# Output stage beside the last MoE: sums, scaling and roots change engine, fetches and list scatters change their waits

## The chip, the cores and the metric

One Trainium2 chip, one of its cores. The metric is the device time of one execution of the program, in microseconds, as the median of several runs; 1389.53 us for the kernel before. TensorE multiplies matrices into PSUM, VectorE and ScalarE work on PSUM and SBUF, GpSimd on SBUF alone; GpSimd also issues the indirect DMAs (gathers and scatters by a list of row numbers), SP the plain ones. Every engine works through its own instructions in order.

## The reference, cut to what matters

A trunk of two layers, 1024 tokens and 16 meta tokens, 1024 channels. Each layer ends in a mixture of experts: every token goes to 2 of 32 experts, and its two weighted results are added to its residual row. After the second layer comes one RMS norm, and the meta tokens are dropped.

```python
h = h + hierarchical_moe(rmsnorm(h, ffn_norm[layer]), ...)      # two experts a token
...
return rmsnorm(h, final_norm)[:, N_META:]

def rmsnorm(x, g):
    y = xf * lax.rsqrt(jnp.mean(xf * xf, axis=-1, keepdims=True) + RMS_EPS)
    return (y * g).astype(x.dtype)
```

## The kernel before, in words

The change lies in the second MoE, the last 400 us of the program. `Moe.run` takes the 32 experts in turn, in passes e = 0 to 32. For each expert, up to 96 tokens' rows are gathered from HBM (`gather`, L905, three passes ahead), turned (L923) and scaled into `xq` (L926), multiplied with gate and up weights (L950 in full precision for one half; L1558 to L1560 for the other, where weights and rows are split into a high and a low part, `wp` and `xT`, by ScalarE at L1553 and VectorE at L1554), passed through silu (ScalarE L974, VectorE L975, tile `hm`), turned again (L984, `ph`, split into `hT`), and multiplied with the down weights (`py`, again L1558 to L1560). VectorE adds the weighted result to the token's row (`rows`, L999), and GpSimd scatters it to `y_d` in HBM (L911), which has two rows a token, one for each of its experts. The passes overlap: pass e holds expert e's gate and up products and expert e-1's turn, down product, L999 and scatter. SP loads the weights into a ring of 17 slots (L895), three a pass, some five experts ahead.

`Out` forms the output rows beside this. Tokens are sorted by the later of their two experts; a list of them is made in passes 0 to 8 by `Router.order` (`later`, `masks`, `sums` on TensorE, `starts`, `places`, `suits`), eight scatters (`place_ids`, L844) and a load (`load_list`, on SP's queue with the weights). The sorted list is cut into seven tiles of 128 tokens. `EARLY_OUT` names the pass at which each tile is due; `suits` counts what is not complete by then, and `again` does everything over where the count is not zero. For tiles 0 to 4, due at pass f:

- `begin(f)`: two gathers fetch the two rows of each token from `y_d` (`fetch`, L1187). The scatters are not ordered among themselves, but the fetch waits for those issued before it.
- `begin(f+1)`: GpSimd adds the two rows (`add`, L1212); `middle(f+1)`: ScalarE squares and sums them (`square`, L1215), ahead of the pass's silu; `end(f+1)`: VectorE takes the root (`root`, L1219 and lines 173 to 183, a start by bits and three steps of refinement).
- `begin(f+2)`: GpSimd multiplies by the gain (`gain`, L1224); `middle(f+2)`: ScalarE multiplies by the root (`scale`, L1227).
- `begin(f+3)`: a scatter writes the tile to the output (`store`, L1197).

Tiles 5 and 6 come in passes 29 to 32. The tokens of the last three experts (`DIRECT`) are not fetched whole: `other` (L1205) fetches their other expert's row and adds it to the row that L999 has just made; `last` and `rest` write these three sets and tile 6 after the final expert.

`begin` stands in a pass right after the gather of three experts ahead, `middle` between the split of `xT` and the second half of the gate and up products, `end` after `hm`. The order of issue in the program is each engine's order of work.

Of the kernel before, what the change touches and what calls it, by code (L numbers as in the profile page):

```python
# [53 lines left out]
EARLY_OUT = (9, 13, 17, 21, 25, 29, 30)  # L54
# [115 lines left out]
def rsqrt_ops(k, y, ms, tmp):  # L170

    V = k.nc.vector
# [162 lines left out]
class Router:  # L335
# [440 lines left out]
    def order(self, psum, c):  # L776
# [9 lines left out]
        def later():  # L786
            V.tensor_tensor(w.rearrange("p (n e) -> p n e", e=NE), self.oh.rearrange("p n j e -> p (n j) e"),
                            k.iota32.unsqueeze(1).to_broadcast([128, 2 * n, NE]), op=OP.mult)
            V.tensor_reduce(self.later.unsqueeze(2), w.rearrange("p (n x) -> p n x", n=n), axis=AX.X, op=OP.max)
# [36 lines left out]
        def suits():  # L826
# [3 lines left out]
            for i, e in enumerate(EARLY_OUT):  # L830
                V.tensor_copy(lim[:, i:i + 1], st[:, e - 1:e])
# [47 lines left out]
class Moe:  # L879
# [121 lines left out]
    def run(self, loads, ahead):  # L1001
# [166 lines left out]
class Out:  # L1168
# [48 lines left out]
    def root(self, i, n=1):  # L1217
        st = self.st[:, :, i:i + n]
        self.k.nc.vector.tensor_scalar(st[:, 1], st[:, 0], 1.0 / D, EPS, op0=OP.mult, op1=OP.add)  # L1219
        for f in rsqrt_ops(self.k, st[:, 2], st[:, 1], st[:, 3]):  # L1220
            f()

    def gain(self, c, n=128):
        self.k.nc.gpsimd.tensor_tensor(c[0][:n], c[0][:n], self.g[:n], op=OP.mult)  # L1224
# [15 lines left out]
    def begin(self, e):  # L1240
        k, r, nc = self.k, self.r, self.k.nc
        later, masks, sums, starts, places, suits = self.order
# [7 lines left out]
        if 5 < e < 6 + DIRECT:  # L1250
            r.load_tokens(e - 6)
# [24 lines left out]
    def middle(self, e):  # L1276

        for f in EARLY_OUT[:-2]:
            if e == f + 1:
                self.square(self.a, 0)  # L1280
            if e == f + 2:
                self.scale(self.a, 0)
        if e == NE - 2:
            self.square(self.a, 0)
        if e == NE - 1:
            self.square(self.b, 1)
            self.square(self.rows(0), 2, CAP)

    def end(self, e):
        k, r = self.k, self.r  # L1290
        later, masks, sums, starts, places, suits = self.order
        if e == 0:
            k.nc.vector.memset(self.st, 1.0)
            k.nc.sync.dma_start(out=self.g, in_=bcast_row(k.A["final_norm"], D))
            later()
        if e == 1:
            masks()
        if e == 2:
            starts()
        if e == 3:  # L1300
            places()
        if e == 4:
            suits()
        if e == 8:
            r.lists()
        if e == 10:
            r.tokens()
        for f in EARLY_OUT[:-1]:
            if e == f + 1:
                self.root(0)  # L1310


    def last(self):

        self.scale(self.a, 0)
# [1334 lines left out]
```

## Time and profile before

| what | us |
|---|---|
| median of 3 runs (1387.86 to 1390.33) | 1389.53 |
| the profiled execution | 1388.98 |
| its span, first to last instruction | 1387.2 |
| TensorE busy in the span | 1279.1 (92%) |
| VectorE | 1071.8 (77%) |
| ScalarE | 756.4 (55%) |
| GpSimd | 391.1 (28%) |

The profile is of one execution. A row names the engine (PE for TensorE, PEld for its weight loads, DVE for VectorE, ACT for ScalarE, POOL for GpSimd, SP for SyncE), the line, the operation and the tiles (out<-in). Granted clock is the share of TensorE's full clock that the chip allowed. Shares of busy time are means over stages with different limits; what the change touches is read from the second MoE, 979 us to the end.

### The profile page before, as it was taken

The page shows a single profiled execution, that of the slowest core. Times are in us where ns is not written, and L with a number is a line of the kernel's source. Part 1 is how long each engine was busy: PE and PEld are TensorE (multiplying, and loading weights), DVE is VectorE, ACT ScalarE, POOL GpSimd, SP SyncE. Part 2 cuts the span into 40 slices and gives each one's busy share as a digit, 9 for nine tenths or more (in the row PEclk, how much of TensorE's full clock was granted, in tenths as well). Part 3 has the DMA queues.
Part 4 walks back from the last instruction along what each step waited for, and adds up shares of the span by engine and source line. Part 5 has one row for each costly group of instructions (what it writes and reads, how often), then busy time and mean ns, then how long its engine had stood idle before and what let it go on. Part 6 is the DMA issues. An engine that isn't in the chain of part 4 may idle for free. (4 is left out here: it accounts for less than half of the span.)

```text
span 1387.2 us, 22810 instructions
## 1 busy us (share of the span) xinstructions
PE 1279.1 (92%) x8029; PEld 1100.5 (79%) x8029; DVE 1071.8 (77%) x2529; ACT 756.4 (55%) x1603; POOL 391.1 (28%) x492
## 2 busy tenths in 40 slices
PE   8979999999997999999999999997899798898883
PEld 6977888888885899899888889896677677686672
DVE  5777888888887776776787676688788688787796
ACT  4435555556555555655665565563555455555553
POOL 0122212121210441122231232213215423323455
PEclk9999999999998999999999999997899999999996
DMA  8927999999963502132010010448596999998632
GB/s 310 396 109 242 371 348 368 352 357 356 351 206 103 196 1 69 48 146 90 20 39 9 12 39 1 167 150 341 192 300 241 385 365 341 355 371 309 220 99 75
DMA packets 81709, 293.12 MB, mean 211 GB/s; under 512 B 22896, under 2 KB 30320, under 8 KB 65074
## 3 DMA queue, kind: packets, MB, share of 16 engines
q1 hardware_dynamic: 63202, 245.54, 48.8%
q0 software_dynamic: 18384, 46.04, 9.9%
q8 instruction: 65, 1.06, 0.3%
q14 instruction: 58, 0.48, 0.1%
HBM read 270.75 MB, written 47.00 MB: 229 GB/s over the span
## 5 line engine op out<-in xcount | busy, mean ns | idle before, releaser
L1558 PE MATMUL gu<-wp,xT 128*96 128x256 f32 x512 | 147.3, 288 | 0.0
L1560 PE MATMUL gu<-wp,xT 128*96 128x256 f32 x512 | 143.4, 280 | 0.0
L1559 PE MATMUL gu<-wp,xT 128*96 128x256 f32 x512 | 143.3, 280 | 0.0
L1554 DVE TENSOR_TENSOR wp<-slotB,wp 128x512 fp32r<-128x512 f32 x160 | 106.9, 690 | 22.5 <-ACT wp L1553 21.6
L1558 PE MATMUL py<-wp,hT 128*96 128x512 f32 x256 | 115.9, 453 | 0.8 <-ACT hT L1553 0.8
L1559 PE MATMUL py<-wp,hT 128*96 128x512 f32 x256 | 104.3, 408 | 8.3 <-DVE wp L1554 8.3
L1560 PE MATMUL py<-wp,hT 128*96 128x512 f32 x256 | 105.3, 411 | 5.3 <-DVE hT L1554 4.9
L1553 ACT ACTIVATE wp<-slotB 128x512 fp32r<-128x512 f32 x160 | 96.0, 626 | 23.8 <-PE py L1560 20.2
L2461 POOL TENSOR_TENSOR hh<-hh,wt 128x512 f32<-128x512 f32 x56 | 72.5, 1294 | 111.4 <-ACT wt L2460 111.4
L1553 ACT ACTIVATE xT<-xq 128x384 fp32r<-128x384 f32 x64 | 33.7, 526 | 111.8 <-DVE xq L926 111.8
L911 POOL DMA_INDIRECT y_d<-xg,di x34 | 35.5, 1043 | 197.9 <-DVE xg L999 188.5
L1558 PEld LDWEIGHTS gu<-wp,xT 128*96 128x96 f32 x512 | 84.9, 166 | 0.1
L1560 PEld LDWEIGHTS gu<-wp,xT 128*96 128x96 f32 x512 | 83.2, 162 | 0.0
L1559 PEld LDWEIGHTS gu<-wp,xT 128*96 128x96 f32 x512 | 82.9, 162 | 0.2
L950 PE MATMUL gu<-slotB,xq 128*96 128x256 f32 x320 | 75.6, 379 | 0.0
L2297 ACT ACTIVATE P<-bank,sm 128x400 f32<-128x400 f32 (+3 forms) x112 | 59.6, 540 | 25.7 <-DVE sm L2287 25.5
L2050 DVE TENSOR_TENSOR T<-bank,T 128x512 fp32r<-128x512 f32 (+2 forms) x112 | 53.6, 495 | 20.8 <-ACT T L2046 19.8
L975 DVE SCALAR_TENSOR_TENSOR hm<-gu,table,hm 96x256 f32<-96x256 f32 x64 | 30.7, 480 | 49.3 <-ACT hm L974 49.3
L926 DVE TENSOR_TENSOR xq<-pt,ffg 128x768 f32<-128x768 f32 (+1 forms) x66 | 61.0, 926 | 9.8 <-PE pt L923 9.8
L1559 PEld LDWEIGHTS py<-wp,hT 128*96 128x96 f32 x256 | 42.7, 167 | 30.8 <-DVE wp L1554 13.7
L2464 DVE SCALAR_TENSOR_TENSOR hh<-bank,ri,hh 128x512 f32<-128x512 f32 x72 | 53.5, 746 | 16.9 <-PE bank L1560 16.4
L1560 PEld LDWEIGHTS py<-wp,hT 128*96 128x96 f32 x256 | 42.7, 167 | 27.1 <-DVE hT L1554 9.4
(444 smaller groups left out, 4060.6 us busy)
## 6 DMA issues: line engine op xcount, KB each, us to landing
slotB<-w_up SPq DMA_DIRECT2D x20, 1024.0 KB, 14.9
slotB<-w_down SPq DMA_DIRECT2D x20, 1024.0 KB, 16.0
slotB<-w_gate SPq DMA_DIRECT2D x20, 1024.0 KB, 16.2
hh<-w_gate SPq DMA_DIRECT2D x11, 1024.0 KB, 14.0
hh<-w_up SPq DMA_DIRECT2D x10, 1024.0 KB, 9.9
hh<-w_down SPq DMA_DIRECT2D x10, 1024.0 KB, 11.4
slotR<-w_gate SPq DMA_DIRECT2D x10, 1024.0 KB, 13.0
slotR<-w_up SPq DMA_DIRECT2D x10, 1024.0 KB, 10.2
```

The costliest lines, as they stand in the source:

```text
L911: return nc.gpsimd.indirect_dma_start(out=self.r.y_d, out_offset=bass.IndirectOffsetOnAxis(ap=didx, axis=0), in_=y[:CAP], in_offset=None, ...
L926: nc.vector.tensor_tensor(x[:, 4 * a:4 * (a + w)].rearrange("p (a b) c -> p a b c", a=w), pt[:, a:a + w].rearrange("p a (b c) -> p a b c", ...
L950: nc.tensor.matmul(gu[:CAP, f * FE:f * FE + FE], lhsT=x[0][:, j], rhs=w[:, j], start=(f == 0 and j == 0), stop=False)
L1553: nc.scalar.activation(dH, src, AF.Copy)
L1554: nc.vector.tensor_tensor(dL, src, dH.bitcast(F32), op=OP.subtract)
L1558: nc.tensor.matmul(out, lhsT=aH, rhs=bH, start=start, stop=False)
L1559: nc.tensor.matmul(out, lhsT=aH, rhs=bL, start=False, stop=False)
L1560: nc.tensor.matmul(out, lhsT=aL, rhs=bH, start=False, stop=stop)
L2050: nc.vector.tensor_tensor(dL, src, dH.bitcast(F32), op=OP.subtract)
L2297: nc.scalar.activation(self.P[hd, qp][a][:, x0:x0 + xe], tt[:, :xe], AF.Exp, bias=sm[:, 3:4], scale=SCALE, accum_out=sm[:, x:x + 1])
L2461: done(end), s.op("G", end + s.LAT, 1170, lambda: nc.gpsimd.tensor_tensor(k.h[i][:, cs], k.h[i][:, cs], x, op=OP.add), lambda end: s.relea ...
L2464: s.op("V", now + s.LAT, 70 + 1.04 * 512, lambda: nc.vector.scalar_tensor_tensor(k.h[i][:, cs], p, self.ri[hd, i], k.h[i][:, cs], op0=OP.m ...
```

## The change

The tiles' sums move from GpSimd to VectorE and stand in `middle(f+1)`; the square moves to `end(f+1)`. The roots of tiles 0 to 6 and of the first direct set move from VectorE to GpSimd, in `begin(f+2)`, written with two-operand operations (14 for a root, where VectorE has 8). Gain and root are multiplied in one VectorE operation in `middle(f+2)`; `gain` and `both` are gone. Each tile's pass f is one later (tiles 0 to 4), and what counts as complete is what the same number of experts had scattered before, so that the fetch no longer depends on the scatter just before it (`apart(x, [self.scat])`). The eight scatters of the list go out together at pass 6 and are declared independent; the list's steps are spread over later passes, and the TensorE step `sums` stands two passes after `masks`. At the end, tile 5 is fetched with tile 6 at pass 30, and the last sets are formed by VectorE, the last two with one root.

```diff
-EARLY_OUT = (9, 13, 17, 21, 25, 29, 30)
+EARLY_OUT = (10, 14, 18, 22, 26, 30, 30)
...
             for i, e in enumerate(EARLY_OUT):
-                V.tensor_copy(lim[:, i:i + 1], st[:, e - 1:e])
+                e -= 1 if i == t - 1 else 2
+                V.tensor_copy(lim[:, i:i + 1], st[:, e:e + 1])
...
         def scatter(y, didx):
             st = self.scatter(y, didx)
+            if out:
+                out.scat = st
...
+            if t < len(EARLY_OUT) - 1:
+                self.apart(x, [self.scat])
             self.got.append(x)
...
-    def root(self, i, n=1):
+    def root(self, i, eng=None, n=1):
+        eng = eng or self.k.nc.gpsimd
...
+        ops[0]()
+        for j in range(3):
+            eng.tensor_tensor(t, y, y, op=OP.mult)
+            eng.tensor_tensor(t, t, ms, op=OP.mult)
+            eng.tensor_scalar(t, t, 3 * _C[j] ** 2, None, op0=OP.subtract)
+            eng.tensor_tensor(y, t, y, op=OP.mult)
 
     def scale(self, c, i, n=128):
-        self.k.nc.scalar.activation(c[0][:n], c[0][:n], AF.Copy, scale=self.st[:n, 2, i:i + 1])
-
-    def both(self, c, i, n=128):
-
         self.k.nc.vector.scalar_tensor_tensor(c[0][:n], c[0][:n], self.st[:n, 2, i:i + 1], self.g[:n], op0=OP.mult, op1=OP.mult)
...
     def begin(self, e):
-        if e == 2:
+        if e == 4:
             sums()
-        for i in range(len(r.tiles)):
-            if e == 4 + i // 4:
-                r.place_ids(i)
         if e == 6:
+            ids = []
+            for i in range(len(r.tiles)):
+                x = r.place_ids(i)
+                self.apart(x, ids)
+                ids.append(x)
+        if e == 8:
             r.load_list()
...
             if e == f:
                 self.fetch(t, self.a)
-            if e == f + 1:
-                self.add(nc.gpsimd, self.a)
             if e == f + 2:
-                self.gain(self.a)
+                self.root(0)
             if e == f + 3:
                 self.store(t, self.a)
-        if e == NE - 3:
+        if e == NE - 2:
             self.fetch(5, self.a)
-        if e == NE - 2:
-            self.add(nc.gpsimd, self.a)
             self.fetch(6, self.b)
             self.other(0, self.rows(0)[0])
         if e == NE - 1:
-            self.add(nc.gpsimd, self.b)
-            self.add(nc.gpsimd, self.rows(0), CAP)
+            self.root(0)
             self.other(1, self.rows(1)[0])
-            self.gain(self.a)
         if e == NE:
-            self.add(nc.gpsimd, self.rows(1), CAP)
+            self.root(1)
             self.other(2, self.rows(2)[0])
+            self.store(5, self.a)
+            self.root(2)
 
     def middle(self, e):
...
+        for f in EARLY_OUT[:-1]:
+            if e == f + 1 and f < NE - 2 or e == f == NE - 2:
+                self.add(V, self.a)
+            if e == f + 2 and f < NE - 2 or e - 1 == f == NE - 2:
                 self.scale(self.a, 0)
...
+    def end(self, e):
+        for x, f in ((0, later), (1, latest), (2, masks), (4, starts), (5, places), (7, suits), (9, r.lists), (11, r.tokens)):
+            if e == x:
+                f()
+        for f in EARLY_OUT[:-1]:
+            if e == f + 1 and f < NE - 2 or e == f == NE - 2:
+                self.square(self.a, 0)
+        if e == NE - 2:
+            self.add(V, self.b)
+        if e == NE - 1:
+            self.add(V, self.rows(0), CAP)
             self.square(self.rows(0), 2, CAP)
...
     def last(self):
-        self.scale(self.a, 0)
-        self.square(self.rows(1), 3, CAP)
-        self.root(1, 3)
+        self.scale(self.b, 1)
 
     def rest(self, scatter):
...
+        self.add(V, d[1], CAP)
+        self.square(d[1], 3, CAP)
         self.add(V, d[2], CAP)
         self.square(d[2], 4, CAP)
         self.scale(d[0], 2, CAP)
+        self.store(6, self.b)
+        scatter()
+        self.root(3, V, 2)
+        self.scale(d[2], 4, CAP)
+        self.scale(d[1], 3, CAP)
```

## Rows read from the trace of the kernel before

**Rows 1.** Busy time by stretch. Each stretch runs from the start of one L999 to that of a later one: two passes in 1013.09:1035.34, 1065.64:1086.94 and 1097.02:1130.81, one in the others; the last runs to the span's end. Columns: length, then busy us and instructions of each engine, the granted clock, the share of the DMA engines' time, GB/s.

```profile
1000.48:1013.09 12.61, 10.35 (x66) 8.53 (x65) 9.98 (x20) 6.88 (x12) 1.97 (x2) 1.00 1.10 250
1013.09:1035.34 22.25, 21.05 (x126) 16.66 (x125) 20.96 (x50) 11.93 (x22) 5.18 (x5) 1.00 0.95 309
1065.64:1086.94 21.30, 20.39 (x126) 16.73 (x125) 17.64 (x31) 11.87 (x22) 11.13 (x10) 1.00 1.00 342
1097.02:1130.81 33.79, 24.32 (x126) 18.70 (x125) 21.71 (x40) 13.94 (x25) 9.63 (x7) 0.85 0.98 372
1150.98:1167.08 16.10, 12.34 (x64) 9.25 (x63) 12.04 (x23) 6.97 (x13) 7.05 (x4) 0.89 0.84 309
1197.34:1214.67 17.33, 13.25 (x64) 9.43 (x63) 12.04 (x22) 6.91 (x13) 7.03 (x4) 0.80 0.86 316
1244.94:1262.99 18.05, 12.18 (x64) 9.12 (x63) 12.06 (x22) 6.97 (x13) 6.62 (x4) 0.91 0.72 262
1293.24:1310.75 17.51, 12.19 (x64) 9.12 (x63) 12.04 (x22) 6.98 (x13) 6.61 (x4) 0.90 0.47 171
1310.75:1320.84 10.09, 10.09 (x64) 8.41 (x63) 8.62 (x15) 6.86 (x12) 3.74 (x3) 1.00 0.33 104
1330.92:1341.38 10.46, 10.46 (x66) 8.50 (x65) 9.95 (x15) 5.93 (x11) 7.51 (x5) 1.00 0.40 123
1341.38:1357.11 15.73, 11.48 (x57) 8.19 (x56) 15.15 (x22) 7.76 (x15) 9.97 (x6) 0.89 0.24 72
1357.11:1369.48 12.37, 7.45 (x25) 4.24 (x23) 11.44 (x20) 6.12 (x13) 8.13 (x5) 0.72 0.26 84
1369.48:1387.20 17.72, 0.00 (x0) 0.00 (x0) 7.95 (x13) 3.45 (x4) 8.97 (x6) 0.57 0.25 78
```

**Rows 2.** The timeline around tile 4, 1283 to 1301 us, each engine's rows picked: start and length in us, engine, line, operation, tiles, shapes, and in brackets the idle time before it and what ended it.

```profile
1283.83 1.04 POOL L1187 DMA_INDIRECT out<-y_d,list  x1 [6.64 <-DMA y_d<-hh,di]
1285.18 0.99 POOL L1187 DMA_INDIRECT out<-y_d,list  x1 [0.31 <-issue]
...
1288.14 1.48 POOL L905 DMA_INDIRECT hh<-h_d,gi  x1 [0.30 <-issue]
1296.26 2.33 POOL L1212 TENSOR_TENSOR out<-out,out 128x1024 f32<-128x1024 f32 x1 [6.63 <-DMA out<-y_d,list]
...
1298.62 1.06 ACT L1215 ACTIVATE out<-out 128x1024 bf16<-128x1024 f32 x1 [4.74 <-POOL out L1212]
...
1299.67 0.45 ACT L974 ACTIVATE hm<-gu,table 96x256 f32<-96x256 f32 x1
...
1300.16 0.48 DVE L975 SCALAR_TENSOR_TENSOR hm<-gu,table,hm 96x256 f32<-96x256 f32 x1 [5.18 <-ACT hm L974]
...
1300.70 0.58 PE L984 MATMUL ph<-cb,hm 96*128 96x96 f32 x2 [4.22 <-DVE ost L1219]
...
1300.93 2.46 DVE L179 SCALAR_TENSOR_TENSOR ost<-ost 128x1 f32<-128x1 f32 x1
...
1301.01 2.35 POOL L1224 TENSOR_TENSOR out<-out,out 128x1024 f32<-128x1024 f32 x1
```

**Rows 3.** The list: TensorE's row at `sums`, from its timeline, and the whole time that GpSimd stood between the list's scatters, from the view of waits (us in total, times, longest).

```profile
1004.24 0.18 PE L805 MATMUL pr<-cnt,tri 128*128 128x32 bf16 x1 [2.26 <-DVE cnt L795]
...
POOL list_d L844 <- DMA list_d<-ids,place: 22.0, 7, 6.3
```

**Rows 4.** From issue to landing (shortest, median, longest) of the gathers of L905 from 990 to 1300 us.

```profile
DMA to landing us min/median/max: 4.4/9.2/15.3
```

**Rows 5.** Single operations from the timelines: VectorE's sum and its product with gain and root near the end; a small GpSimd operation; a VectorE operation alone and the same beside GpSimd's L600; the last scatter of the program.

```profile
1370.85 1.22 DVE L1212 TENSOR_TENSOR xgh<-xgh,xg 96x1024 f32<-96x1024 f32 x1
1371.99 1.27 DVE L1231 SCALAR_TENSOR_TENSOR out<-out,ost,out 96x1024 f32<-96x1024 f32 x1
...
938.92 0.25 POOL L614 TENSOR_TENSOR r<-v,b 128x8 f32<-128x8 f32 x1
939.23 0.19 POOL L612 CAST b<-r 128x8 bf16<-128x8 f32 x1
...
938.75 0.35 DVE L693 TENSOR_TENSOR ro<-cb,rank 128x192 bf16<-128x192 f32 x1
...
940.04 1.62 POOL L600 TENSOR_TENSOR vi<-oh,b 128x384 bf16<-128x384 f32 x2
...
941.08 0.79 DVE L693 TENSOR_TENSOR ro<-cb,rank 128x192 bf16<-128x192 f32 x1
...
1380.20 0.91 POOL L1197 DMA_INDIRECT out<-xgh,ti  x1 [0.31 <-issue]
```

**Rows 6.** A plain pass, from the timelines of VectorE, ScalarE and TensorE, 1283 to 1289 us.

```profile
1283.16 1.27 DVE L999 SCALAR_TENSOR_TENSOR xg<-py,table,xg 96x1024 f32<-96x1024 f32 x1
1284.35 0.55 DVE L1554 TENSOR_TENSOR xT<-xq,xT 128x384 fp32r<-128x384 f32 x1
1285.21 0.48 DVE L975 SCALAR_TENSOR_TENSOR hm<-gu,table,hm 96x256 f32<-96x256 f32 x1 [0.31 <-ACT hm L974]
...
1285.07 1.14 ACT L1553 ACTIVATE wp<-kT 128x512 fp32r<-128x512 f32 x2
...
1286.23 0.33 PE L984 MATMUL ph<-cb,hm 96*128 96x96 f32 x2
...
1288.59 0.39 PE L1560 MATMUL py<-wp,hT 128*96 128x512 f32 x1
```

More of the change, by code (lines that the diff above doesn't have):

```diff
@@ L838, in suits @@
             V.tensor_copy(self.bad, b[:, 8:9])
-        return later, masks, sums, starts, places, suits
+        return later, latest, masks, sums, starts, places, suits
     def place_ids(self, i):
-        self.k.nc.gpsimd.indirect_dma_start(
+        return self.k.nc.gpsimd.indirect_dma_start(
             out=self.list_d, out_offset=bass.IndirectOffsetOnAxis(ap=self.place[:, i:i + 1], axis=0),
@@ L1215, in square @@
         self.k.nc.scalar.activation(c[-1].bitcast(BF16)[:n, :D], c[0][:n], AF.Square, accum_out=self.st[:n, 0, i:i + 1])
-    def root(self, i, n=1):
+    def root(self, i, eng=None, n=1):
+        eng = eng or self.k.nc.gpsimd
         st = self.st[:, :, i:i + n]
[L1219 to L1224, printed above, removed]
+        ss, ms, y, t = (st[:, j] for j in range(4))
+        eng.tensor_scalar(ms, ss, 1.0 / D, EPS, op0=OP.mult, op1=OP.add)
+        ops = rsqrt_ops(self.k, y, ms, t, eng)
+        if eng is self.k.nc.vector:
+            for f in ops:
+                f()
+            return
+        ops[0]()
[4 more added lines that the diff above has]
+            eng.tensor_tensor(y, t, y, op=OP.mult)
     def scale(self, c, i, n=128):
-        self.k.nc.scalar.activation(c[0][:n], c[0][:n], AF.Copy, scale=self.st[:n, 2, i:i + 1])
-    def both(self, c, i, n=128):
         self.k.nc.vector.scalar_tensor_tensor(c[0][:n], c[0][:n], self.st[:n, 2, i:i + 1], self.g[:n], op0=OP.mult, op1=OP.mult)
@@ L1241, in begin @@
         k, r, nc = self.k, self.r, self.k.nc
-        later, masks, sums, starts, places, suits = self.order
-        if e == 2:
+        later, latest, masks, sums, starts, places, suits = self.order
+        if e == 4:
             sums()
-        for i in range(len(r.tiles)):
-            if e == 4 + i // 4:
-                r.place_ids(i)
         if e == 6:
+            ids = []
[4 more added lines that the diff above has]
+        if e == 8:
             r.load_list()
-        if 5 < e < 6 + DIRECT:
-            r.load_tokens(e - 6)
+        if 8 <= e < 8 + DIRECT:
+            r.load_tokens(e - 8)
         for t, f in enumerate(EARLY_OUT[:-2]):
@@ L1282, in middle @@
+        for f in EARLY_OUT[:-1]:
+            if e == f + 1 and f < NE - 2 or e == f == NE - 2:
+                self.add(V, self.a)
+            if e == f + 2 and f < NE - 2 or e - 1 == f == NE - 2:
                 self.scale(self.a, 0)
-        if e == NE - 2:
-            self.square(self.a, 0)
         if e == NE - 1:
             self.square(self.b, 1)
-            self.square(self.rows(0), 2, CAP)
[L1289 to L1310, printed above, removed]
+    def end(self, e):
+        k, r, V = self.k, self.r, self.k.nc.vector
+        later, latest, masks, sums, starts, places, suits = self.order
+        if e == 0:
+            V.memset(self.st, 1.0)
+            k.nc.sync.dma_start(out=self.g, in_=bcast_row(k.A["final_norm"], D))
+        for x, f in ((0, later), (1, latest), (2, masks), (4, starts), (5, places), (7, suits), (9, r.lists), (11, r.tokens)):
+            if e == x:
+                f()
+        for f in EARLY_OUT[:-1]:
[5 more added lines that the diff above has]
+            self.add(V, self.rows(0), CAP)
+            self.square(self.rows(0), 2, CAP)
@@ L1313, in last @@
     def last(self):
-        self.scale(self.a, 0)
-        self.square(self.rows(1), 3, CAP)
-        self.root(1, 3)
+        self.scale(self.b, 1)
     def rest(self, scatter):
-        nc, V, r = self.k.nc, self.k.nc.vector, self.r
-        b, d = self.b, [self.rows(i) for i in range(DIRECT)]
-        self.store(5, self.a)
-        self.gain(b)
-        scatter()
-        self.gain(d[0], CAP)
+        V, r = self.k.nc.vector, self.r
+        d = [self.rows(i) for i in range(DIRECT)]
+        self.add(V, d[1], CAP)
@@ L1327, in rest @@
+        self.square(d[1], 3, CAP)
         self.add(V, d[2], CAP)
-        self.scale(b, 1)
         self.square(d[2], 4, CAP)
         self.scale(d[0], 2, CAP)
-        self.both(d[1], 3, CAP)
-        self.root(4)
-        self.both(d[2], 4, CAP)
-        self.store(6, b)
-        for i in (1, 0, 2):
+        self.store(6, self.b)
[3 more added lines that the diff above has]
+        self.scale(d[1], 3, CAP)
+        for i in (0, 2, 1):
             self.keep(d[i], r.ti[:CAP, 0, i:i + 1])
@@ L1346, in again @@
                 self.square(c, 0)
-                self.root(0)
-                self.both(c, 0)
+                self.root(0, nc.vector)
+                self.scale(c, 0)
                 nc.sync.dma_start(out=self.out[0, t * 128:(t + 1) * 128], in_=c[0])
```

10 lines of the change are left out of this document (4 added, 6 removed).

## The prediction

> **What bounds the kernel now.** I read the last stage, the 32 experts of the second MoE, pass by pass. First the busy times by stretch, each stretch running from one start of the row update L999 to a later one. A pass with nothing beside it takes 10.09 us and TensorE is busy in all of it, at a granted clock of 1.00 [rows 1]: TensorE sets the pace, and VectorE, busy 8.62 us, has 1.5 us to spare. The passes that carry the early output stand out: five stretches, six passes, 33.79 + 16.10 + 17.33 + 18.05 + 17.51 = 102.78 us against 60.54 at the plain pace, so 42.2 us lost on tiles 0 to 4. The list costs 2.5 us in the first stretch and 1.1 in 1065.64 to 1086.94. The last stretches, 15.73, 12.37 and 17.72 us, hold tiles 5 and 6 and the three direct experts.
>
> Then the timeline of one such tile shows how 7.4 us are lost [rows 2]. The two fetches are issued late (GpSimd stood 6.64 us for the last scatter's landing) and the sum on GpSimd starts 12.4 us after the first. ScalarE stands 4.74 us for that sum in front of the silu, VectorE 5.18 us for the silu, TensorE 4.22 us for the turn. Then GpSimd's multiplication by the gain (2.35 us) holds a VectorE operation of the root for 2.46 us. The slow clock adds the rest: 0.80 to 0.91 on average in these stretches, between its two levels (1.2 and 2.4 GHz), after TensorE had stood for 4 us and more; the stretch with the list's 2.26 us stop kept 1.00 [rows 1, 3].
>
> **The change part by part**, against the profiled execution of 1388.98 us (span 1387.2 and 1.8 around it); the median of the three runs is 0.55 above it.
>
> *The list.* The sums on TensorE now come two passes after the masks, not at once, so the stop of 2.26 us goes [rows 3]; the masks themselves still cost VectorE 1.5 us, nearly within its spare: -2.3 of 2.5. Two steps, starts and places, move two passes on and bring their cost along: the stretch 1013.09 to 1035.34 is 2.07 us above two plain passes, before and after. The eight scatters no longer wait for each other (22.0 us of GpSimd's time [rows 3]); they occupy GpSimd for eight times 1.3 us in one go, which delays that pass's row scatter by 3 us and the gather behind it, wanted three passes later. The late gather that made 1.1 us in the stretch from 1065.64 goes: -1.1. On SP the load of the list is issued two passes later, after the scatters have landed, so the weight loads behind it keep moving.
>
> *Fetches.* They are issued one pass later but no longer wait for the last scatter. I count from a pass's L999. The previous scatter, a gather and then the two fetches go out from +1.55 on, in about 5 us. Now the pair alone took 12.4 us from its first issue to the sum [rows 2]; the slowest gather queued behind a pair took 15.3 us, and it is issued 4.3 us after the first fetch [rows 2, 4], so four transfers take up to 19.6. The pair then lands at +19 to +21.2; VectorE wants it at two passes plus 1.7, +21.9. It just fits; I take 0.3 us a tile, with ends 0 and 3.
>
> *The sum and the square, pass f+1.* 1.22 us of VectorE [rows 5] right after the xT split, which in a plain pass is followed by a gap of 0.31 us [rows 6]. The update hm ends 0.8 us later; the turn on TensorE had 0.5 us in hand (hm ends at +2.53, ph starts at +3.07), so 0.3 late. The square (1.05 us, the distance from its start to the silu's in [rows 2]) now stands on ScalarE behind the silu and waits for the sum, to about +4.0; the copies wp that began at +1.91 begin there, hT's high half comes at +5.4 and its low half at +6.3, where the third product of py wanted it at 5.4. I take 1.1 us; ends 0.3 (only the turn) and 1.9 (all of the 1.22 + 1.05 above the 0.31 gap).
>
> *The scaling, pass f+2.* 1.27 us of VectorE [rows 5] at the same place: the turn alone, 0.35 us; ends 0 and 1.0. It takes the place of GpSimd's gain and ScalarE's scale.
>
> *The roots on GpSimd.* 14 small operations at the 0.3 us pitch of [rows 5] are 4 us, begun when the square is done (+4.2); the scaling wants them at a pass plus 2.8. While GpSimd ran two operations that read SBUF, a VectorE operation of 0.35 us took 0.79 [rows 5]: they hold each other up. By that each small operation may cost VectorE its 0.2 us, 2.8 us a tile; nine or so fall on the wp splits, and VectorE has about 1.3 us in hand there. I take 0.6; ends 0 and 2.8.
>
> A tile so costs 1.1 + 0.35 + 0.6 + 0.3 = 2.35 us, five 11.8, and 42.2 - 11.8 = **-30.4**. No stop is left that is as long as the 2.26 us after which the clock stayed at 1.00.
>
> *The end.* Stretch 1330.92: the GpSimd sum that lengthened it leaves, -0.4. Stretch 1341.38: VectorE was held by two GpSimd sums and a gain; now it does two sums itself, and the second waits for the fetch of tile 6, the fourth of five gathers issued together: about 1.5 us of waiting, 2.2 above plain in all, 12.3 us: -3.4. Next stretch: the gains and the root over three columns leave, but two squares, a scaling and a sum stand before hT: 12.2, -0.2. After the last L999: now 17.72, with the last scatter issued at +10.7 [rows 5]. Afterwards two sums, a scaling, a root over two columns (2.2) and two scalings, 1.3 + 2.4 + 1.25 + 2.2 + 2.5, then the last scatter at about +9.9: -0.8. Ends for the three together: +4 and -8.
>
> *Weights.* They don't bind: the DMA share has fallen to 0.47 and 0.33 by 1293 to 1321 [rows 1], some 30 us before the last expert's pass. The shorter passes use up part of that.
>
> **Sum:** -2.3 - 1.1 - 30.4 - 0.4 - 3.4 - 0.2 - 0.8 = -38.6, so 1350.4 by the profiled execution and 1351 by the median.
>
> **Rivals.**
> 1. *The roots come late.* If every small operation first lets a 0.6 us split of VectorE go by, 14 take 11.2 us, to +15.4, where the scaling wants them at +12.9: 2.5 us of VectorE standing, five times, **1363**. For it: the 0.79 us in [rows 5], and splits that follow each other without a gap through most of a pass. Against: xq, hm and L999 read PSUM, and about 5 operations run before or between the splits. The Trainium skill, SBUF — State Buffer, section "SBUF: two separate sides", says that VectorE with two SBUF inputs and GpSimd take one port pair in turn, for a whole instruction, the other blocked; by that rule the time would be this rival's, and the 2.46 us in [rows 2] agrees with it.
> 2. *The rows come late.* The margin of a tile is 0.7 to 2.9 us, and with shorter passes the DMA engines, at a share of 0.84 to 1.0 in the stretches up to 1214 [rows 1], are asked for more. If the pair lands 3 us late, or the fetch still waits for the last scatter, VectorE itself stands: five times 3, **1366**. The Trainium skill, DMA: Bandwidth & Descriptors, section "Queues, rings and completion order", says that an engine serves its queues in turn; by that a backlog of weights need not lengthen GpSimd's transfers, which no run here shows alone.
> 3. *Slower.* The wait for fetched rows moves from GpSimd and ScalarE to VectorE, which works in order and feeds every product. A stop of 5.18 us there cost 7.4 [rows 1, 2], 1.4 times. The whole gain, 38.6 or 7.7 us a tile, is gone when VectorE stands 5.5 us per tile, the pair landing after +27 where [rows 2, 4] give at most +21.2. Beyond that, **1395**.
> 4. *Everything hides.* Root, landing and most of the square cost nothing: 0.8 us a tile, **1344**. For it: VectorE's 1.5 us to spare. Against: ScalarE's copies stand behind the square.
>
> **How the numbers follow.** Forecast 0.62, rival 1 0.13, rival 2 0.13, rival 4 0.08, rival 3 0.03, nothing to measure 0.01 (0.2% is what a measurement of this kernel can tell from no change). The predicted time is the forecast's, 1351. For the forecast alone, all low ends together would give 1333 (five times 2.05 and 8 less), the high ends without the two rivals' own 1362 (five times 1.45 and 4 more); they won't all fall on one side, and half of either way is 1342 to 1357. The two late rivals reach to 1366: the range 1342 to 1366 leaves out less than 2 in 10. Faster 0.96, same 0.01, slower 0.03.
>
> **What would show it.** Right: L999 to L999 11 to 12 us in pass f+1 and about 10.7 in f+2 for every tile, a granted clock of 1.00 there; no wait of VectorE at the sum for the fetch; GpSimd's last root operation ahead of the scaling; no stop before the list's sums. Wrong: VectorE waiting for DMA at the sum (rival 2) or for GpSimd at the scaling (rival 1), a TensorE stop of over 3 us with a slower clock behind it, or the last three stretches of [rows 1] together above 43 us, where 41.4 is forecast.

## The result and the profile after

The changed kernel takes **1348.28 us** (median of 4 runs, 1344.79 to 1349.53) against 1389.40 of the kernel before beside it: ratio **0.9701, 95% interval 0.9681 to 0.9721**. 1351.0 was forecast, in 1342 to 1366. The profiled execution took 1349.53, its span 1347.7, 39.5 us under the span before.

First the busy times by stretch, from one start of the row update (now L1002) to the next, as in [rows 1]:

```profile
999.67:1009.75 10.08, 10.08 (x64) 8.40 (x63) 9.13 (x15) 6.76 (x12) 1.96 (x2) 1.00 0.95 339
1041.18:1052.55 11.37, 10.57 (x64) 8.34 (x63) 10.71 (x25) 5.93 (x11) 6.72 (x7) 1.00 1.02 371
1052.55:1065.11 12.56, 10.53 (x64) 8.23 (x63) 8.47 (x15) 5.80 (x11) 5.63 (x6) 1.00 0.96 306
1105.50:1116.51 11.01, 10.76 (x64) 8.16 (x63) 10.29 (x19) 6.96 (x13) 8.11 (x14) 1.00 1.01 362
1116.51:1126.96 10.45, 10.30 (x64) 8.32 (x63) 9.56 (x15) 5.94 (x11) 5.22 (x6) 1.00 1.01 380
1230.41:1241.43 11.02, 10.78 (x64) 8.16 (x63) 9.57 (x15) 6.97 (x13) 8.19 (x14) 1.00 1.03 364
1272.06:1283.07 11.01, 10.77 (x64) 8.17 (x63) 9.58 (x15) 6.97 (x13) 8.18 (x14) 1.00 0.68 250
1283.07:1293.52 10.45, 10.30 (x64) 8.32 (x63) 9.55 (x16) 5.93 (x11) 4.12 (x5) 1.00 0.58 233
1303.61:1314.50 10.89, 10.14 (x56) 7.35 (x55) 9.84 (x15) 7.61 (x14) 8.08 (x13) 1.00 0.31 104
1314.50:1326.53 12.03, 7.35 (x27) 4.52 (x25) 8.04 (x12) 4.31 (x10) 9.05 (x21) 0.73 0.12 33
1326.53:1347.72 21.19, 0.00 (x0) 0.00 (x0) 9.08 (x17) 2.30 (x4) 11.75 (x21) 0.58 0.31 104
```

The reader is to see four things. Every tile costs the same two passes, 11.01 and 10.45 us, at a granted clock of 1.00, where before the first of them took 16 to 18 us (tiles 1 to 4; 33.79 for both passes of tile 0) at 0.80 to 0.91 [rows 1]: above the plain 10.09, tiles 0 to 4 cost 6.4 us in place of 42.2. The first pass, 12.61 in [rows 1], is 10.08. One pass is long that was not forecast, 12.56: it is the one in which the last of the list's eight scatters go out (GpSimd issues them from 1046.57 to 1057.17). I call this the stop at the scatters. And the last stretch has *grown*, from 17.72 us [rows 1] to 21.19.

The account of 39.5: the stages ahead 0.8, the list (first ten passes) 0.8, tiles 0 to 4 35.8, from tile 5 on 2.1.

The timeline around tile 4, engines' rows picked as in [rows 2]:

```profile
1273.62 0.47 ACT L977 ACTIVATE hm<-gu,table 96x256 f32<-96x256 f32 x1 [0.91 <-PE gu L1559]
1275.01 1.06 ACT L1222 ACTIVATE out<-out 128x1024 bf16<-128x1024 f32 x1 [0.93 <-DVE out L1219]
...
1273.72 1.21 DVE L1219 TENSOR_TENSOR out<-out,out 128x1024 f32<-128x1024 f32 x1
1274.85 0.47 DVE L978 SCALAR_TENSOR_TENSOR hm<-gu,table,hm 96x256 f32<-96x256 f32 x1
1278.20 2.70 DVE L1553 TENSOR_TENSOR wp<-slot,wp 128x512 fp32r<-128x512 f32 x4
1284.73 1.27 DVE L1242 SCALAR_TENSOR_TENSOR out<-out,ost,out 128x1024 f32<-128x1024 f32 x1
...
1275.38 0.38 PE L987 MATMUL ph<-cb,hm 96*128 96x96 f32 x2
...
1277.10 0.36 POOL L1228 TENSOR_SCALAR ost<-ost 128x1 f32<-128x1 f32 x1
1281.73 0.63 POOL L1238 TENSOR_SCALAR ost<-ost 128x1 f32<-128x1 f32 x1
1283.55 0.19 POOL L1239 TENSOR_TENSOR ost<-ost 128x1 f32<-128x1 f32 x1
```

No bracket at VectorE's sum (L1219) or scaling (L1242): rows and root are there before it asks. The silu (L977) waits for nothing of the tile; the turn (L987) follows without a stop. GpSimd's root runs from 1277.10 to 1283.74, 6.6 us for 14 operations, each 0.2 us alone and up to 0.63 beside VectorE's copies, and ends 1.0 us before the scaling.

The tail, VectorE's rows and then GpSimd's (VectorE's first is of the stretch ahead of the last):

```profile
1324.53 1.28 DVE L1242 SCALAR_TENSOR_TENSOR xg<-xg,ost,out 128x1024 f32<-128x1024 f32 x1 [1.48 <-POOL ost L1239]
...
1329.88 1.22 DVE L1219 TENSOR_TENSOR xgh<-xgh,xg 96x1024 f32<-96x1024 f32 x1 [0.94 <-DMA xgh<-y_d,ti]
1333.71 1.28 DVE L1242 SCALAR_TENSOR_TENSOR hh<-hh,ost,out 96x1024 f32<-96x1024 f32 x1 [2.61 <-POOL ost L1239]
...
1325.17 1.58 POOL L1212 DMA_INDIRECT xgh<-y_d,ti  x1 [0.67 <-issue]
1328.14 0.85 POOL L1228 TENSOR_SCALAR ost<-ost 128x1 f32<-128x1 f32 x1
1329.89 1.29 POOL L1238 TENSOR_SCALAR ost<-ost 128x1 f32<-128x1 f32 x1
1333.48 0.19 POOL L1239 TENSOR_TENSOR ost<-ost 128x1 f32<-128x1 f32 x1
1340.65 0.91 POOL L1204 DMA_INDIRECT out<-out,ti  x1 [0.30 <-issue]
```

VectorE waits 2.61 us for the second of the two roots that GpSimd does in the last pass; the first (1319.41 to 1324.50) held up tile 6's scaling by 1.48 and put off the fetch at 1325.17, for which VectorE waits 0.94. The last scatter goes out at +14.1 of the stretch; it was +10.7 before [rows 1, 5].

### The profile page after: what moved, and what is told of

Its sections match the earlier page's. It is cut to its first block, busy times and chain, and to the rows that moved or that the text cites. A ratio compares the mean times of both kernels' runs of the same rounds, so it can differ in the third digit from the quotient of the medians.

```text
span 1347.7 us, 22878 instructions
## 1 busy us (share of the span) xinstructions
PE 1267.6 (94%) x8029; PEld 1091.1 (81%) x8029; DVE 1055.0 (78%) x2490; ACT 748.0 (55%) x1595; POOL 401.9 (30%) x587
## 5 line engine op out<-in xcount | busy, mean ns | idle before, releaser
L1557 PE MATMUL py<-wp,hT 128*96 128x512 f32 x256 | 112.7, 440 | 5.2 <-ACT hT L1552 5.2
L1552 ACT ACTIVATE wp<-slotB 128x512 fp32r<-128x512 f32 x160 | 96.0, 626 | 23.8 <-PE py L1559 20.2
L1559 PE MATMUL py<-wp,hT 128*96 128x512 f32 x256 | 102.9, 402 | 2.1 <-DVE hT L1553 2.0
L914 POOL DMA_INDIRECT y_d<-xg,di x34 | 38.9, 1144 | 212.2 <-DVE xg L1002 205.7
L1558 PE MATMUL py<-wp,hT 128*96 128x512 f32 x256 | 101.5, 396 | 0.7 <-DVE wp L1553 0.7
L2463 DVE SCALAR_TENSOR_TENSOR hh<-bank,ri,hh 128x512 f32<-128x512 f32 x72 | 53.5, 747 | 16.8 <-PE bank L1559 16.4
L977 ACT ACTIVATE hm<-gu,table 96x256 f32<-96x256 f32 x64 | 30.0, 469 | 61.4 <-PE gu L1559 61.4
L1553 DVE TENSOR_TENSOR wp<-hh,wp 128x512 fp32r<-128x512 f32 x82 | 54.8, 689 | 11.8 <-ACT wp L1552 11.4
L2459 ACT ACTIVATE wt<-bank,ri 128x512 f32<-128x512 f32 x56 | 38.5, 688 | 41.7 <-PE bank L1559 34.6
```

The source lines that it names most:

```text
L914: return nc.gpsimd.indirect_dma_start(out=self.r.y_d, out_offset=bass.IndirectOffsetOnAxis(ap=didx, axis=0), in_=y[:CAP], in_offset=None, ...
L1552: nc.scalar.activation(dH, src, AF.Copy)
L1553: nc.vector.tensor_tensor(dL, src, dH.bitcast(F32), op=OP.subtract)
L1557: nc.tensor.matmul(out, lhsT=aH, rhs=bH, start=start, stop=False)
L1558: nc.tensor.matmul(out, lhsT=aH, rhs=bL, start=False, stop=False)
L1559: nc.tensor.matmul(out, lhsT=aL, rhs=bH, start=False, stop=stop)
```

## The experiments

My theory: tiles 0 to 4 gain because nothing late stands between a fetch and the silu any more. Its rivals: that one part (the independence of the fetch, or VectorE's sum) is the gain, or that the roots are the price. "Tiles" is what the passes of tiles 0 to 4 take above 10.09 us each, from the profile; ratios are to the kernel before beside it. The recorded text under each edit is what was expected of the run, with its own theory A and rival B.

| kernel | median us | ratio, 95% | tiles us |
|---|---|---|---|
| before | 1389.40 | 1 | 42.2 |
| changed | 1348.28 | 0.9681 to 0.9721 | 6.4 |
| changed again | 1347.10 | 0.9652 to 0.9701 | 6.4 |
| fetch waits | 1353.67 | 0.9714 to 0.9748 | 9.6 |
| sum on GpSimd | 1350.26 | 0.9674 to 0.9727 | 6.4 |
| both of these | 1360.71 | 0.9753 to 0.9811 | 18.1 |
| square in front | 1354.73 | 0.9711 to 0.9765 | 11.8 |
| roots on VectorE | 1351.11 | 0.9693 to 0.9737 | 11.7 |
| gain on GpSimd | 1355.01 | 0.9720 to 0.9759 | 14.7 |
| before + fetch | 1374.66 | 0.9840 to 0.9908 | 19.6 |
| before + sum | 1389.27 | 0.9965 to 1.0002 | 41.7 |
| old list | 1355.50 | 0.9709 to 0.9755 | 6.4 |
| tail roots on VectorE | 1344.32 | 0.9636 to 0.9684 | 6.4 |
| tail and list mended | 1343.49 | 0.9624 to 0.9673 | 6.4 |

**The fetch waits again.** (Tile 5's fetch too, which the edit includes.)

```diff
-            if t < len(EARLY_OUT) - 1:
-                self.apart(x, [self.scat])
```

> The changed kernel, but the fetches of tiles 0 to 4 wait again for the last scatter. In the changed kernel the pair of tile 1 is issued 5.5 and 6.9 us after that scatter and the sum comes 14.8 us after the first of the pair; with a landing some 9 us behind the scatter the pair goes out about 4 us later. Theory A (the gain came from everything that stood between the fetch and the silu, and there are a few us in hand): 0 to 1 us a tile, 1348 to 1353 us, VectorE waiting under 1 us at the sum. Rival B (the independence of the fetch is the gain, rival 2 of the prediction): VectorE stands 3 us or more at each sum, 1363 us or more.

Theory A held for the tiles in the main: +3.2 us over five, 1.5 of it tile 3's, shown here, where VectorE's wait is above the 1 us expected. The median, 1353.67, is just above the 1353 expected; tile 5, which the expectation left out, cost 3 to 4 us more (its pass 15.0 us in place of 10.9 and 12.1 in the changed kernel's two profiles). GpSimd's row, then VectorE's:

```profile
1219.18 1.02 POOL L1192 DMA_INDIRECT out<-y_d,list  x1 [6.18 <-issue]
...
1232.19 1.23 DVE L1217 TENSOR_TENSOR out<-out,out 128x1024 f32<-128x1024 f32 x1 [1.40 <-DMA out<-y_d,list]
```

GpSimd stands 6.18 us (the row names no releaser; at tiles 1 and 4 it is the scatter, after 6.36 and 5.71), about as long as in [rows 2], and VectorE only 1.40: the old wait alone is small, because the sum and the square now ask later.

**The sum on GpSimd.**

```diff
+            if e == f + 1:
+                self.add(nc.gpsimd, self.a)
...
-            if e == f + 1 and f < NE - 2 or e == f == NE - 2:
+            if e == f == NE - 2:
                 self.add(V, self.a)
```

> The changed kernel, but the sums of tiles 0 to 4 are on GpSimd again, in its queue ahead of pass f+1 as before. Theory A (the pair now lands before pass f+1 begins, so GpSimd has summed it by then, and what was costly was the late pair, not the engine): ScalarE doesn't wait, the lock of 2.3 us falls on VectorE's copies, 0 to 1 us a tile either way, 1345 to 1353 us. Rival B (the sum on VectorE is a main part of the gain): VectorE loses 2.3 us and ScalarE waits again, 2 to 3 us a tile, 1358 to 1363 us.

Theory A: 1350.26, the tiles' sum unchanged. The stretches of tiles 2 and 3, and GpSimd's rows, show that it is two cases:

```profile
1188.05:1198.15 10.10, 10.10 (x64) 8.40 (x63) 8.68 (x14) 6.86 (x13) 8.66 (x15) 1.00 0.92 322
1228.79:1240.82 12.03, 10.56 (x64) 8.25 (x63) 8.52 (x14) 6.97 (x13) 9.43 (x14) 1.00 0.96 354
...
1186.64 2.88 POOL L1219 TENSOR_TENSOR out<-out,out 128x1024 f32<-128x1024 f32 x1 [4.57 <-DMA out<-y_d,list]
...
1230.01 2.73 POOL L1219 TENSOR_TENSOR out<-out,out 128x1024 f32<-128x1024 f32 x1 [7.19 <-DMA out<-y_d,list]
```

Tile 2's pair lands 1.4 us before the pass begins, and GpSimd's sum is free (10.10; VectorE's costs 0.92); tile 3's lands 1.2 us after it, and the pass takes 12.03, with ScalarE 1.97 us in wait for the sum, where theory A had no wait. The 10.10 shows one thing more: tile 2's square and all but the end of its root on GpSimd (1192.12 to 1198.82) lie in that pass and cost it nothing.

**Both undone together.** (The two edits above, tile 5 left as changed.)

> The changed kernel with two parts undone together: the fetches of tiles 0 to 4 wait for the last scatter, and their sums are on GpSimd. Each alone cost 0 to 4 us. Theory A (the two remedies stand in for each other: with a late pair, the sum of 2.4 us in GpSimd's queue, ahead of pass f+1, holds the square behind the silu and the copies behind that): pair complete some 13 us after L1002 of pass f, 3 us into pass f+1, the sum to 5.5, ScalarE held for up to 4 us, 2 to 4 us a tile more: 1356 to 1366 us. Rival B (their costs add): 1349 to 1354 us.

Theory A: 11.7 us over the tiles, where the two alone add 3.2. ScalarE's and TensorE's rows in tile 3's pass:

```profile
1242.61 1.06 ACT L1222 ACTIVATE out<-out 128x1024 bf16<-128x1024 f32 x1 [2.65 <-POOL out L1219]
...
1245.06 0.73 PE L1559 MATMUL py<-wp,hT 128*96 128x512 f32 x1 [1.99 <-ACT hT L1554]
```

The late pair and GpSimd's 2.34 us in a row reach ScalarE, behind it `hT`, then TensorE; the granted clock of that stretch is 0.88 and the pass 13.90 us. Early rows or a sum asked for late: one of the two must be there.

**The square ahead of the silu.**

```diff
                 self.add(V, self.a)
+                if f < NE - 2:
+                    self.square(self.a, 0)
...
-            if e == f + 1 and f < NE - 2 or e == f == NE - 2:
+            if e == f == NE - 2:
                 self.square(self.a, 0)
```

> The changed kernel, but the square of tiles 0 to 4 is issued on ScalarE ahead of the silu again, not behind it. Theory A (the place of the square is a part of the gain of its own: ScalarE now has the sum to wait for before the silu, and VectorE's hm and TensorE's turn stand behind it): 1 to 2 us a tile more, 1351 to 1358 us, with VectorE waiting about 1.5 us for the silu at hm in pass f+1. Rival B (ScalarE does the same work in the pass either way): within 1 us of 1346.

Theory A, 1.1 us a tile. VectorE waits 1.62 us at `hm`, as expected, for a silu that stands behind the square:

```profile
1235.83 0.48 DVE L978 SCALAR_TENSOR_TENSOR hm<-gu,table,hm 96x256 f32<-96x256 f32 x1 [1.62 <-ACT hm L977]
```

**Roots on VectorE.**

```diff
             if e == f + 2:
-                self.root(0)
+                self.root(0, nc.vector)
```

> The changed kernel, but the roots of tiles 0 to 4 are on VectorE, 1.25 us each at the start of pass f+2. Theory A (GpSimd's small operations are hidden: the root ends 1 us before the scaling and the passes show no cost for it): the 1.25 us are added to the scaling's in pass f+2, 0.5 to 1.3 us a tile, 1351 to 1355 us. Rival B (GpSimd's small operations hold VectorE as long as VectorE's own would take): no change, 1348, or faster by up to 2 us.

Theory A in size: 5.3 us over five tiles. In place not quite: they fall in pass f+1 (12.06 in place of 11.02), since `begin(f+2)` stands ahead of the copies that VectorE makes before its next L1002. So GpSimd's roots save 1.1 us a tile.

**The gain on GpSimd.**

```diff
                 self.root(0)
+                self.gain(self.a)
...
-            if e == f + 2 and f < NE - 2 or e - 1 == f == NE - 2:
+            if e == f + 2 and f < NE - 2:
+                self.scale_act(self.a, 0)
+            if e - 1 == f == NE - 2:
                 self.scale(self.a, 0)
```

(`gain` and `scale_act` are the kernel before's: GpSimd multiplies by the gain, ScalarE by the root.)

> The changed kernel, but the scaling of tiles 0 to 4 is done as before, the gain by GpSimd (behind its root) and the root's factor by ScalarE at the place where VectorE's scaling stood. Theory A: GpSimd's 2.3 us start when the root has ended, about 1.0 us before the scaling's place, so ScalarE stands some 1.5 us, scales for 1.3 and the silu comes late: 1 to 2.5 us a tile more, 1353 to 1361 us. Rival B (the scaling's engine does not matter once the rows come early): within 1 us of 1348.

Theory A: 1.7 us in each pass f+2. ScalarE stands for GpSimd's product in front of the silu:

```profile
1248.18 1.15 ACT L1245 ACTIVATE out<-out,ost 128x1024 f32<-128x1024 f32 x1 [2.37 <-POOL out L1242]
```

**The kernel before with the early fetch alone.**

```diff
-EARLY_OUT = (9, 13, 17, 21, 25, 29, 30)
+EARLY_OUT = (10, 14, 18, 22, 26, 29, 30)
...
-                V.tensor_copy(lim[:, i:i + 1], st[:, e - 1:e])
+                e -= 2 if i < t - 2 else 1
+                V.tensor_copy(lim[:, i:i + 1], st[:, e:e + 1])
...
+            if t < len(EARLY_OUT) - 2:
+                self.apart(x, [self.scat])
```

> The kernel before with one part of the change: tiles 0 to 4 are fetched one pass later, from rows two experts back, without waiting for the last scatter. Sum, gain, square, root, scaling, list and end as before. Theory A (the late pair is what stood behind the stops): GpSimd's sum ends before pass f+1 begins, the 5.18 us wait of VectorE for the silu goes, what stays is the square in front of the silu and the gain's lock, 2.5 to 3.5 us a tile in place of 8.4: 25 to 30 us gained, 1360 to 1365 us. Rival B (the engines that sum and scale are the gain): under 10 us gained, 1380 us or more.

Neither: 16.4 us by the medians. The tiles did as theory A said in part: 42.2 fell to 19.6, 3.9 each, 2.25 more stands in the pass ahead of the first. Another pass near the list, 17.1 us long in this profile, took 6 of it back (with the next pass 27.2 us, 21.3 before); ScalarE stands 5.89 us there for a releaser that the profile does not name. What is left of tile 3, from the rows of GpSimd, ScalarE and VectorE:

```profile
1247.46 2.40 POOL L1217 TENSOR_TENSOR out<-out,out 128x1024 f32<-128x1024 f32 x1 [5.20 <-DMA out<-y_d,list]
...
1249.89 1.06 ACT L1220 ACTIVATE out<-out 128x1024 bf16<-128x1024 f32 x1 [1.02 <-POOL out L1217]
...
1252.20 2.65 DVE L179 SCALAR_TENSOR_TENSOR ost<-ost 128x1 f32<-128x1 f32 x1
```

The wait for the sum has fallen from 4.74 us [rows 2] to 1.02; the gain's hold on VectorE's root, 2.65, is as it was.

**The kernel before with the sum on VectorE and the square behind the silu alone.**

```diff
-            if e == f + 1:
-                self.add(nc.gpsimd, self.a)
             if e == f + 2:
+                self.root(0)
                 self.gain(self.a)
...
             if e == f + 1:
-                self.square(self.a, 0)
+                self.add(self.k.nc.vector, self.a)
...
-            if e == f + 1:
+            if e == f + 1 and f < NE - 3:
+                self.square(self.a, 0)
+            if e == f + 1 and f == NE - 3:
                 self.root(0)
```

> The kernel before with the other half of the remedy alone: sums of tiles 0 to 4 on VectorE in pass f+1, the square behind the silu, the root on VectorE one pass later; fetches as before, waiting for the last scatter, and gain, scale, list and end as before. The edits undone from the changed kernel cost 3.2 us over its tiles (fetch), 5.4 (root) and 8.5 (gain). Theory A (early fetch, and a sum that nothing before the silu waits for, each remove most of the stops): tiles cost some 23 us in place of 42.2, so 16 to 21 us gained, 1370 to 1375 us. Rival B (with the late pair VectorE only stands where ScalarE stood): under 8 us gained, 1382 us or more.

**My theory failed here.** I expected 16 to 21 us; the ratio is 0.9984 (0.9965 to 1.0002), the tiles 41.7. It is not rival B either, but for tile 0, where VectorE waits 5.31 us at the sum: for tiles 1 to 4 it waits 0 to 1.11 (0.81 for tile 3). VectorE's, GpSimd's and TensorE's rows of tile 3's pass show a third thing:

```profile
1247.93 3.04 DVE L179 SCALAR_TENSOR_TENSOR ost<-ost 128x1 f32<-128x1 f32 x1
...
1248.61 2.34 POOL L1224 TENSOR_TENSOR out<-out,out 128x1024 f32<-128x1024 f32 x1
...
1251.83 0.74 PE L1560 MATMUL py<-wp,hT 128*96 128x512 f32 x1 [3.43 <-DVE wp L1555]
...
1241.67:1259.46 17.79, 13.24 (x63) 9.45 (x62) 13.85 (x23) 6.96 (x13) 4.32 (x3) 0.81 0.82 309
```

GpSimd's gain begins while VectorE is in the middle of the root, an operation of 0.22 us takes 3.04, the copies and `hT` stand behind it, TensorE stops for 3.43 us, and the granted clock is 0.81 (last row, the stretch). It is alike in tiles 1 to 4: such an operation takes 2.88 to 3.05 us, and TensorE stops for 3.33 to 3.50. By these rows a stop of VectorE for GpSimd's product has taken the place of the stop for the sum, and the whole price came back; no run moved the gain as well to try it. So costs of edits undone one by one from the changed kernel do not add up from the other side.

**The list as before.**

```diff
-        if e == 4:
+        if e == 2:
             sums()
+        for i in range(len(r.tiles)):
+            if e == 4 + i // 4:
+                r.place_ids(i)
         if e == 6:
...
-        if e == 8:
             r.load_list()
...
-        for x, f in ((0, later), (1, latest), (2, masks), (4, starts), (5, places), (7, suits), (9, r.lists), (11, r.tokens)):
+        for x, f in ((0, later), (0, latest), (1, masks), (2, starts), (3, places), (4, suits), (8, r.lists), (10, r.tokens)):
```

(The block under `if e == 6`, not shown, loses the eight independent scatters; the loads of the tokens' numbers come two passes earlier too.)

> The changed kernel with the list as before: masks and their sums on TensorE two passes earlier and one after the other, scatters that wait for each other over two passes, loads two passes earlier. Theory A (the list's part of the gain is the 2.26 us stop before the sums and little else): 2 to 3.5 us more than the changed kernel without its stop, 1347 to 1351 us, the first pass 12.6 us again. Rival B (the place of the list costs or gains nothing, since the stop only moves): the same as the changed kernel within 1 us.

More than either: 8.4 us. The first ten passes cost 7.9 us above plain against 2.4 in the changed kernel's second profile: 5.5. The first pass took 14.31 us and not the 12.6 expected: the stop of 2.26 us is there as in [rows 3], but where the kernel before kept a granted clock of 1.00 [rows 1], it is 0.88 here. The other part lies 240 us later: the pass of tiles 5 and 6 took 15.92 us against 12.05. TensorE's row and the stretch of the first pass, the view of SP's waits (us in total, times, longest), then three stretches:

```profile
1003.39 0.18 PE L807 MATMUL pr<-cnt,tri 128*128 128x32 bf16 x1 [2.26 <-DVE cnt L797]
...
999.62:1013.93 14.31, 12.05 (x66) 9.44 (x65) 9.99 (x20) 6.87 (x12) 1.96 (x2) 0.88 1.00 217
...
SPq L853 <- DMA list_d<-ids,place: 20.2, 3, 14.9
...
1045.60:1055.60 10.00, 10.00 (x64) 8.32 (x63) 8.63 (x15) 5.93 (x11) 4.21 (x5) 1.00 0.80 318
1055.60:1065.60 10.00, 10.00 (x63) 8.33 (x62) 8.55 (x14) 5.93 (x11) 4.62 (x5) 1.00 0.12 33
1065.60:1075.60 10.00, 8.79 (x51) 6.78 (x49) 8.57 (x14) 5.93 (x11) 7.77 (x7) 1.00 0.83 252
```

SP stands 20.2 us at the load of the list, waiting for the scatters, with the weights queued behind it: the DMA share falls to 0.12 (0.05 in the kernel before, 0.94 in the changed one in that stretch). The last weight load is issued at 1282.2 us in place of 1268.6, 8 us more than the passes themselves are late; in the two passes before tile 5's sum the DMA share is still 0.73 and 0.71 (0.60 in both in the changed kernel), and VectorE waits 2.65 and 1.75 us for the rows of tiles 5 and 6, against 0 and 2.17. That the weights make the rows late is read from these rows, and was not tried by itself.

**The tail's roots on VectorE.**

```diff
-            self.root(1)
             self.other(2, self.rows(2)[0])
             self.store(5, self.a)
-            self.root(2)
...
     def last(self):
+        self.root(1, self.k.nc.vector, 2)
         self.scale(self.b, 1)
```

> The changed kernel, but the two roots that GpSimd does in the last pass (tile 6 and the first direct expert) are one root over two columns on VectorE, ahead of tile 6's scaling. In the changed kernel VectorE waits 1.48 us for the first of them, 0.94 for a fetch that GpSimd issues behind it, and 2.61 for the second. Theory A: these 5.0 us go and about 2.2 us of VectorE come, 3 us less in the last stretch, 1343 to 1346 us, and the fetch of the third direct expert is issued about 5 us earlier. Rival B (the end is set by GpSimd's queue of stores or by the landing of rows, and the waits only move): within 1 us of the changed kernel.

Theory A: 1344.32; the last stretch 17.25 in place of 21.19. The rows of VectorE and of GpSimd:

```profile
1329.04 1.22 DVE L1219 TENSOR_TENSOR xgh<-xgh,xg 96x1024 f32<-96x1024 f32 x1
1330.17 1.28 DVE L1242 SCALAR_TENSOR_TENSOR hh<-hh,ost,out 96x1024 f32<-96x1024 f32 x1
...
1323.23 0.97 POOL L1212 DMA_INDIRECT xgh<-y_d,ti  x1 [3.73 <-issue]
1337.29 0.91 POOL L1204 DMA_INDIRECT out<-out,ti  x1 [0.30 <-issue]
```

All three waits are gone and VectorE's two-column root fits where it waited before: 3.9 us in the stretch, with none lost in the one ahead (12.11 for 12.03). The fetch left only 2 us earlier, not 5: GpSimd stands 3.73 us before it, for what the profile does not show.

**The changed kernel again, and both mended** (the tail's edit, and the list's eight scatters four in pass 6 and four in pass 7):

> The changed kernel once more, on the same chip as the next two. In its first profile the pass after the eight scatters of the list took 2.47 us too long; profiles of later variants with the same list show it in three of seven. Theory A (the stop comes in some executions only): the median stays within 1346 to 1350 us, and the pass takes either 10.1 or 12.6 to 12.8 us. Rival B (it belongs to the list's new place): the pass is over 12 us again.

Theory A: 1347.10, and the pass of the last scatters takes 10.08 us this time. The same kernel shows the stop once and once not.

> The changed kernel with the root over two columns on VectorE in the last pass, and with the list's eight scatters four in one pass and four in the next, in place of eight in one. Theory A (the tail's waits are worth 3 to 4 us, and a burst of eight scatters makes the stop of the pass after it): 3 to 6 us under the changed kernel on the same chip, no pass over 10.2 us right after the scatters. Rival B (the stop has another cause): 3 to 4 us under it, the stop still there in some profiles.

1343.49, 3.6 us under the changed kernel beside it; the two intervals overlap (0.9624 to 0.9673, 0.9652 to 0.9701), the profile has the 3.6 us in the last stretch (17.24 for 20.84). It is the best version that I ran. It shows no stop at the scatters, but neither do five other profiles with eight in a burst, so it does not tell theory A from B.

## Why the prediction was right, and where not

The number is 2.7 us from the median; its terms were less good. The tiles gave 5.4 us more than forecast, the list and the end together 5.3 less; that these cancel is luck.

- **Tiles, -30.4 forecast, -35.8 measured.** The mechanism held. Sum and square: 1.1 a tile forecast, 0.92 measured; scaling: 0.35, 0.36. The root, 0.6, and the landing, 0.3, show no cost (tile 2's 10.10 us in the run with the sum on GpSimd holds nearly all of a root). The step that failed is that a small GpSimd operation "may cost VectorE its 0.2 us": VectorE's four copies beside the root took 2.70 us, and 2.66 with no root beside them (the row below, from the pass of the scatters); the GpSimd operations were the ones that stretched, to 0.63. The Trainium skill, SBUF — State Buffer, section "SBUF: two separate sides", has one of the two blocked for the other's whole instruction; the 1.29 us of a GpSimd operation beside VectorE's 1.22 us sum, and VectorE's 3.04 beside GpSimd's 2.34, agree: each ends with the other engine's operation. By that rule I gave rival 1 to the tiles; there it was GpSimd that gave way, and its root still had 1.0 us.

```profile
1060.42 2.66 DVE L1553 TENSOR_TENSOR wp<-slotR,wp 128x512 fp32r<-128x512 f32 x4 [0.16 <-issue]
```

- **The landing.** I had the fetches out from +1.55 on; those of tiles 1 to 4 left 2.9 to 3.6 us later, since the buffer was still being read by the tile's predecessor's store (GpSimd's wait before L1192, 2.91 to 3.60 us), a wait that I did not name. The pair was in time all the same at all five sums, because the pair took less than the 19.6 us that I allowed: where the landing can be read, in the run with the sum on GpSimd, tile 3's pair is there 13.4 us after its first issue (1216.62 to 1230.01). Rival 2's price of 3 us a tile was too high: with the wait put back, tile 3 stands 1.40.
- **The clock.** No stop of TensorE over 1.5 us is left in the tiles, and the stretches are at 1.00, as forecast. But I argued from the length of a stop, and that alone does not decide: the 2.26 us after which the clock stayed at 1.00 [rows 1, 3] were followed by 0.88 in the run with the old list, and with fetch and sum both undone, stops of 2.41, 2.80, 1.99 and 2.21 us in the passes of tiles 1 to 4 went with 0.88, 1.00, 0.88 and 1.00. Nor had TensorE stood for 4 us and more in every slow stretch before: it was 2.81 us in 1150.98:1167.08 and 2.82 in 1197.34:1214.67.
- **The list, -3.4 forecast, -0.8 measured** in the first profile and -3.4 in the second (10.08 us where the first has 12.56). The terms were about right; the 2.5 us stop was not among them. Of the nine profiles with the eight scatters in a burst four show it (12.6 to 12.8 us) and five do not; in the first, ScalarE waits 2.05 us for products whose recorded end lies earlier. Its cause stays open. What I left at nothing was SP: I wrote that the weights "keep moving" and gave it no price. With the list undone SP stands 20.2 us, and the pass of tiles 5 and 6 is 3.9 us longer; that the one makes the other is read, not tried.
- **The end, -4.8 forecast, -2.1 measured.** Stretches forecast at 12.3 and 12.2 took 10.89 and 12.03: tile 6's rows came 1.0 us late where I had 1.5, and the second profile has 12.05 for the first of them. The failing step is the last stretch, 16.9 forecast and 21.19 measured. I counted VectorE's operations and left out that two of its inputs now came from GpSimd in line with that engine's fetches and stores: 1.48, 0.94 and 2.61 us of waiting. That is rival 1, in the one place where I had not looked for it; the run with these roots on VectorE takes 3.9 of it back. By the prediction's own signs the end was wrong: the last three stretches take 44.1 us together (44.6 in the second profile), above the 43 set there, VectorE waits for GpSimd at a scaling, and TensorE has a stop of 3.24 us in the stretch of 12.03, at a granted clock of 0.73.
- **Rival 3** did not come: VectorE waits for no row of tiles 0 to 4. **Rival 4** came halfway: the root and the landing hid, as it said, while sum and square together still cost 0.92; a tile costs 1.28 us, where the forecast had 2.35 and this rival 0.8. The tiles were nearer to it than to the forecast.

Undone one at a time, the parts of the tiles' change cost 3.2 (fetch), 0 (sum), 5.4 (square), 5.3 (root) and 8.3 (gain); fetch and sum together 11.7. With that pair it makes about 31 of the 35.8, but the two runs from the side of the kernel before give 22.6 and 0.5: what a part is worth depends on which other stop is still there. Why before + fetch has the 17.1 us pass is open too.

## What to carry to other kernels

A stop has several sufficient causes when late rows, a slow sum and a blocked engine follow each other in one pass: removing one may give nothing (before + sum) or half (before + fetch), so cost the pass as a chain and ask what stands next. Small work moved to an idle engine was free where its deadline was a pass away; in the tail the same root that hid five times became a 2.6 us wait. And a DMA that waits at the head of a queue shared with the weights may be paid for much later, where the stream's lead is used up; here that is read from the rows and was not tried alone.

## What the runs showed that I had not expected

- Beside VectorE's copies GpSimd's one-column operations took 0.5 to 0.6 us for 0.2, while the copies kept their 0.65 to 0.70; one multiplication on 128x1024 by GpSimd (2.34 us) stretched a VectorE operation of 0.22 us to 3.04.
- A GpSimd sum whose rows are there is free (10.10 us), VectorE's own costs 0.92 in every tile; late rows turn it round (12.03 and 11.02).
- After a stand of SP of 20.2 us for eight small scatters the weight stream ended later by 8 us beyond the passes' own delay; the pass that took 3.9 us longer came 240 us later.
- The same stop of TensorE of 2.26 us left the granted clock of its pass at 1.00 in the kernel before (12.61 us) and at 0.88 in the run with the old list (14.31 us); one of 1.99 us went with 0.88, one of 2.80 with 1.00.
